# A decoder trunk on one core: S5 tables in other PSUM banks, six norm halves by sums of ones, four smaller moves

## The chip, the cores and the metric

The kernel runs on one core of a Trainium2 chip. The metric is device time in microseconds for one execution. TensorE (PE) has a sequencer and a weight loader of its own (PEld); VectorE (DVE), ScalarE (ACT) and GpSimd (POOL) run beside it, each in its own order, and SyncE (SP) starts most transfers.

## The reference, cut to what matters

Two layers over a sequence of 1024 tokens with 1024 channels, all float32. Each layer is a mixer and a cross-attention over 256 memory tokens, with an RMS norm ahead of each and a residual behind it; a last norm ends the trunk.

```python
def rms_norm(x, g):
    xf = x.astype(jnp.float32)
    y = xf * lax.rsqrt(jnp.mean(xf * xf, axis=-1, keepdims=True) + EPS)
    return (y * g.astype(jnp.float32)).astype(x.dtype)
...
def spatial_gating(u, v, ln_g, ln_b, w_s, b_s):
...
    vn = ((vf - mu) * lax.rsqrt(var + EPS) * ln_g.astype(jnp.float32) + ln_b.astype(jnp.float32)).astype(v.dtype)
```

The first layer's mixer runs dilated attention (16 heads, three patterns) and trailing pools, gates both, and projects 2048 channels back to 1024. The second layer's mixer runs a spatial gating unit (C) and an S5 state-space layer with a GLU (D), gates both, and projects 1536 channels back.

## The kernel before

Everything is held transposed: channels on the 128 partitions, tokens along the free dimension, in two halves of 512 tokens (h is 0 or 1). A float32 product is made of three matmuls on split operands: ACT rounds the operand to its high part (`hilo`, `split`), DVE subtracts to get the low part, and PE adds high x high, high x low and low x high (`mm3`, L206 to L208). So each weight tile `wst` that SP loads becomes `wh` by ACT and `wl` by DVE, and each activation tile becomes a pair.

The stages follow one another on PE: the fold of the memory tokens into the cross-attention weights and the load of x (0 to 200 us); AB, the projections and the attention of the first layer with the pools at its end (200 to 929); its output projection `out_proj` (929 to 1110); cross-attention 0 (to 1290); CD (to 1724); its output projection (to 1860); cross-attention 1 and the last norm (to 2057). While AB runs, a side generator, `s5_prep`, makes the tables of S5 for four groups d: POOL builds a factor W in some 11 us of tensor operations, PE transposes it in two halves (L1154), ACT copies each half out of PSUM to `s5wz` (L1155), PE multiplies it with 16 columns (L1160), DVE masks that to `ktr` (L1165), POOL's queue stores both. The recorded order of each engine is fixed when the kernel is built, and an engine waits for semaphores in that order.

PSUM has four tags with two banks each: `mm`, `s`, `o`, `t`. The tag `mm` holds projections; in AB, `s` holds scores (L536), `t` the transposes of the probabilities (L567, L570), `o` the attention's values (L593, L605). A bank comes free when the engine that reads it is done.

The norm of the next stage is collected while a stage ends. POOL adds squares into `acc` (`norm_sq`). `later` then queues two steps that `flush` runs between projections: `norm_cols` sums over the channels with four matmuls of one column each (L297, a float32 matmul, recorded twice) and gets the factors with ten operations of four columns on DVE (L300 to L306). For CD the factor is wanted along the free dimension too, so `norm_rep` makes four diagonal blocks on DVE (L313), spreads them with a float32 matmul of 512 columns (L314) and copies them to `R` by ACT (L317). In CD, `xd` (L1314) multiplies each projection by `R`.

In `out_proj`, `g_load` (L746) fetches the gated mixer output that was stored to DRAM, and `hilo` splits it to `gr`. In `cd_main` eight tiles `vh` are normalised (L1359) ahead of the gates `ug` (L1367). At the end `norm_rep` gets the factors of the last 256 tokens and `finish` (L285) applies them.

Of the kernel before, what the change touches and what calls it, by code (L numbers as in the profile page):

```python
# [16 lines left out]
EPS = 1e-6  # L17
# [81 lines left out]
class Prog:  # L99
# [164 lines left out]
    def later(s, st, h):  # L264

        s.todo.append(lambda: None)

        def end():
            if st["g"] in (G_X0, G_X1):
                s.norm_cols(st, s.Rt[:, 4 * h:4 * h + 4], 4)  # L270
            else:
                s.norm_rep(st, s.Rt[:, 4 * h:4 * h + 4], s.R[h])
        s.todo.append(end)
# [15 lines left out]
    def norm_cols(s, st, out, n):  # L289
# [10 lines left out]
        V.tensor_scalar(v, p[:, :n], 1.0 / 1024, EPS, op0=ALU.mult, op1=ALU.add)  # L300

        V.tensor_scalar(y.bitcast(mybir.dt.int32), v.bitcast(mybir.dt.int32), -0.5, 1597463007.0, op0=ALU.mult, op1=ALU.add)
        for i in range(3):
            V.tensor_tensor(q, y, y, op=ALU.mult)
            V.scalar_tensor_tensor(q, v, -0.5, q, op0=ALU.mult, op1=ALU.mult)
            V.scalar_tensor_tensor(out if i == 2 else y, q, 1.5, y, op0=ALU.add, op1=ALU.mult)  # L306

    def norm_rep(s, st, Rt, R, n=4):

        s.norm_cols(st, Rt, n)  # L310
        p, d = s.ps("t"), s.u("diag")
        for j in range(n):
            s.nc.vector.tensor_scalar(d[:, 128 * j:128 * j + 128], s.ident, Rt[:, j:j + 1], None, op0=ALU.mult)  # L313
        s.nc.tensor.matmul(p[:, :128 * n], lhsT=s.onef, rhs=d[:, :128 * n], start=True, stop=True)  # L314
        if R is None:
            return p[:, :128 * n]
        s.nc.scalar.activation(R, p[:, :128 * n], AF.Copy)  # L317
# [110 lines left out]
    def load_x(s):  # L428

        s.xg = {}  # L430
        for h in range(2):
# [6 lines left out]
            s.norm_rep(st, s.Rt[:, 4 * h:4 * h + 4], s.R[h])  # L438
# [3 lines left out]
    def proj(s, key, h, held):  # L442
# [6 lines left out]
        if h == 1:  # L449
            s.free(key)  # L450
            del held[key]
            s.flush()
# [224 lines left out]
    def ab_main(s):  # L677
# [15 lines left out]
    def ab_pool(s, gi):  # L693
# [36 lines left out]
        H, L = s.get(key)  # L730
        for d2 in range(2):
# [18 lines left out]

    def out_proj(s, name, KT, gain, get_x, tag):

        s.gr = {}
        todo = [(k, h) for h in range(2) for k in range(KT)]
# [41 lines left out]
    def cross(s, l, gain, tag, save=True):  # L796
# [60 lines left out]
        for si, (h, c0, w) in enumerate(segs):  # L857
            st = {"g": gain}
            fin = {}
            for ct in range(8):  # L860
# [35 lines left out]
                else:  # L896
                    s.norm_sq(st, ct, x, w, last=(ct == 7))
                    nc.scalar.activation(x, x, AF.Copy, scale=s.gains[:, 8 * gain + ct:8 * gain + ct + 1])
                yield 1
# [16 lines left out]
    def s5_prep(s):  # L916
# [224 lines left out]
        zero = s.keep("zero", 128)  # L1141
        V.memset(zero, 0.0)
        for d in range(4):
# [7 lines left out]
            for j in range(2):  # L1151
                p = s.ps("t")
# [5 lines left out]
            p = s.ps("s")  # L1158
# [10 lines left out]
            nc.gpsimd.dma_start(s.s5k[d][128:], zero)  # L1169
# [135 lines left out]
    def cd_main(s):  # L1305
# [52 lines left out]
        for tt in range(8):  # L1358
            V.tensor_scalar(vh[tt], vh[tt], mv[:, 2 * tt:2 * tt + 1], rs[:, tt:tt + 1], op0=ALU.subtract, op1=ALU.mult)  # L1359
        wt, bias = s.sgu  # L1360
        for ct in range(8):
            uu, gg = {}, {}
            for j, dst in ((ct, uu), (8 + ct, gg)):
                for h in range(2):
# [197 lines left out]
```

## Time and profile before

| | |
|---|---|
| three runs | 2055.49, 2062.45, 2062.06 us (median 2062.06) |
| profiled execution | 2059.17 us |
| its span | 2057.4 us, mean granted PE clock 0.997 |
| busy PE, DVE, ACT, POOL | 2020.7, 1102.9, 800.2, 539.9 us |
| PE idle in the span | 36.7 us |

The profiled execution lies between the runs, and 1.8 us of it lie outside the span. Every difference is worked out within the span. PE's busy time counts the pipelined length of each matmul, so back-to-back matmuls of 512 columns start 0.23 us apart though each is shown as 0.39 us.

### The profile page before, as it was taken

How to read it: one execution, taken by the hardware profiler on the slowest of the kernel's cores; microseconds unless marked ns; L12 is line 12 of the kernel's file. 1: busy time of each engine (PE TensorE's matmuls, PEld its weight loads, DVE VectorE, ACT ScalarE, POOL GpSimd, SP SyncE). 2: the span in 40 equal slices, each digit the busy share in tenths (PEclk: the TensorE clock that was granted, in tenths of full speed). 3: DMA queues.
4: the chain of work that ended last, by engine and by line, in shares of the span. 5: the costliest groups of instructions: out<-in, count | busy, mean ns of one | idle time of the engine just before them, and what ended most of it. 6: DMA issues, size and time to landing. Idle time of an engine off the chain costs nothing.

```text
span 2057.4 us, 31828 instructions
## 1 busy us (share of the span) xinstructions
PE 2020.7 (98%) x12350; PEld 1680.1 (82%) x12350; DVE 1102.9 (54%) x1987; ACT 800.2 (39%) x1618; POOL 539.9 (26%) x802
## 2 busy tenths in 40 slices
PE   8999999999999999999999999999999999999998
PEld 7999877777777777888888888888888887888887
DVE  6665055655566675555544555444654334555544
ACT  7666134455344453114433444122221122434453
POOL 5332007922334274221111013221221101210013
PEclk9999999999999999999999999999999999999999
DMA  8889202213122122136533145523321226541142
GB/s 297 300 276 321 93 22 75 73 52 113 54 74 89 59 77 98 70 115 237 186 133 130 42 159 179 164 82 98 121 90 67 80 84 197 197 154 62 67 159 83
DMA packets 129159, 258.68 MB, mean 126 GB/s; under 512 B 12784, under 2 KB 58992, under 8 KB 129008
## 3 DMA queue, kind: packets, MB, share of 16 engines
q1 hardware_dynamic: 86608, 189.52, 27.4%
q0 software_dynamic: 13440, 43.53, 5.7%
q10 hardware_dynamic: 28960, 23.60, 3.6%
q8 instruction: 97, 1.59, 0.3%
q14 instruction: 54, 0.44, 0.1%
HBM read 193.16 MB, written 63.44 MB: 125 GB/s over the span
## 4 chain that ended last, share of the span: by engine, by line
PE 86%; DVE 5%; ACT 2%; issue 1%; DMA 1%; POOL 1%; DVEq 0%; ACTq 0%; POOLq 0%
PE ps_mm L206 13%; PE ps_mm L207 13%; PE ps_mm L208 13%; PE ps_s L207 4%; PE ps_s L208 4%; PE ps_s L206 4%; PE ps_o L208 3%; PE ps_o L207 3%; PE ps_o L206 3%; PE ps_s L536 2%; PE ps_mm L1340 1%; PE ps_mm L1338 1%; PE ps_mm L1339 1%; PE ps_o L593 1%; PE ps_mm L472 1%
## 5 line engine op out<-in xcount | busy, mean ns | idle before, releaser
L181 DVE TENSOR_TENSOR wl<-wst,wh 128x1024 fp32r<-128x1024 f32 (+1 forms) x263 | 346.2, 1330 | 101.9 <-ACT wh L180 97.6
L206 PE MATMUL ps_mm<-xg,wh 128*128 128x512 f32 x928 | 369.9, 399 | 1.3 <-DVE ug L1367 1.0
L207 PE MATMUL ps_mm<-xg,wh 128*128 128x512 f32 x928 | 362.7, 391 | 0.0
L208 PE MATMUL ps_mm<-xg,wl 128*128 128x512 f32 x928 | 362.1, 390 | 0.0
L180 ACT ACTIVATE wh<-wst 128x1024 fp32r<-128x1024 f32 (+1 forms) x263 | 262.6, 1017 | 105.0 <-PE ps_mm L207 84.7
L206 PEld LDWEIGHTS ps_mm<-xg,wh 128*128 128x128 f32 x928 | 174.4, 188 | 47.8 <-issue 10.3
L208 PEld LDWEIGHTS ps_mm<-xg,wl 128*128 128x128 f32 x928 | 174.3, 188 | 36.9
L207 PEld LDWEIGHTS ps_mm<-xg,wh 128*128 128x128 f32 x928 | 174.7, 188 | 33.8 <-issue 0.2
L243 POOL TENSOR_TENSOR acc<-acc,sq 128x512 f32<-128x512 f32 (+1 forms) x81 | 102.3, 1263 | 214.9 <-ACT sq L239 207.8
L226 ACT ACTIVATE xg<-x,gains 128x512 fp32r<-128x512 f32 x64 | 46.2, 722 | 243.5 <-DVE x L782 186.5
L548 ACT ACTIVATE P<-P,mx 128x192 f32<-128x192 f32 (+7 forms) x128 | 66.1, 517 | 155.2 <-DVE mx L547 154.7
L580 ACT ACTIVATE PTr<-ps_t 128x128 f32<-128x128 f32 (+2 forms) x192 | 40.6, 268 | 120.3 <-DVE PT L576 117.9
L543 DVE TENSOR_TENSOR P<-ps_s,cst 128x320 f32<-128x320 f32 (+7 forms) x128 | 65.5, 549 | 21.2 <-PE ps_s L536 9.7
L227 DVE SCALAR_TENSOR_TENSOR xg<-x,gains,xg 128x512 fp32r<-128x512 f32 x64 | 51.7, 807 | 42.9 <-ACT xg L226 42.9
L1367 DVE TENSOR_TENSOR ug<-ps_mm,R 128x512 f32<-128x512 f32 x32 | 22.1, 689 | 90.4 <-PE ps_mm L208 90.3
L576 DVE TENSOR_TENSOR PT<-ps_t,cst 128x256 f32<-128x256 f32 (+1 forms) x128 | 46.4, 400 | 44.4 <-PE ps_t L570 38.6
L207 PE MATMUL ps_s<-gr,wh 128*128 128x512 f32 x168 | 65.6, 390 | 2.1 <-DVE gr L214 2.1
L206 PE MATMUL ps_s<-gr,wh 128*128 128x512 f32 x168 | 65.5, 390 | 1.2 <-ACT gr L213 1.2
L208 PE MATMUL ps_s<-gr,wl 128*128 128x512 f32 x168 | 65.4, 389 | 0.0
L550 ACT ACTIVATE P<-P,den 128x192 f32<-128x192 f32 (+7 forms) x128 | 61.4, 511 | 6.2 <-DVE den L549 6.0
L239 ACT ACTIVATE sq<-x 128x512 f32<-128x512 f32 (+1 forms) x77 | 44.8, 582 | 42.6 <-DVE x L890 37.9
L536 PE MATMUL ps_s<-kk,q 64*32 64x256 f32 (+7 forms) x2048 | 58.4, 332 | 0.9 <-DVE ktr L1165 0.9
(424 smaller groups left out, 4841.8 us busy)
## 6 DMA issues: line engine op xcount, KB each, us to landing
wst<-w_ab SPq DMA_DIRECT2D x40, 512.0 KB, 3.6
wst<-w_out_ab SPq DMA_DIRECT2D x32, 512.0 KB, 4.2
wst<-vsc SPq DMA_DIRECT2D x32, 512.0 KB, 4.4
wst<-w_kv SPq DMA_DIRECT2D x31, 512.0 KB, 7.0
wst<-w_cd SPq DMA_DIRECT2D x24, 512.0 KB, 3.3
wst<-w_out_cd SPq DMA_DIRECT2D x32, 384.0 KB, 3.4
wst<-w_q SPq DMA_DIRECT2D x16, 512.0 KB, 8.4
msc<-mo ACTq DMA_DIRECT2D x32, 256.0 KB, 6.4
```

The lines of the kernel that those rows point to most:

```text
L180: s.last_hi = s.nc.scalar.activation(H[:, :w], t[:, :w], AF.Copy)
L181: s.nc.vector.tensor_tensor(L[:, :w], t[:, :w], H[:, :w], op=ALU.subtract)
L206: s.nc.tensor.matmul(ps, lhsT=lh, rhs=rh, start=(i == 0), stop=False)
L207: s.nc.tensor.matmul(ps, lhsT=lh, rhs=rl, start=False, stop=False)
L208: s.nc.tensor.matmul(ps, lhsT=ll, rhs=rh, start=False, stop=(i == n - 1))
L227: nc.vector.scalar_tensor_tensor(L, x, g, H, op0=ALU.mult, op1=ALU.subtract)
L243: nc.gpsimd.tensor_tensor(st["acc"][:, :n], st["acc"][:, :n], q[:, :n], op=ALU.add)
L536: i = nc.tensor.matmul(p[e][32 * r:32 * r + 32, c], lhsT=q[rows[e], 128 * b + 32 * r:128 * b + 32 * r + 32], rhs=x, start=True, stop=True)
L543: nc.vector.tensor_tensor(t[:, :n], p[e][:, :n], s.cst[:, m0:m0 + n], op=ALU.add)
L548: j = nc.scalar.activation(t[:, :m], t[:, :m], AF.Exp, bias=mx, accum_out=den)
L550: k = nc.scalar.activation(t[:, :m], t[:, :m], AF.Copy, scale=den)
L576: nc.vector.tensor_tensor(PT[b // 2, e][:, c0 + 128 * j0:c0 + 256].rearrange("p (j i) -> p j i", i=128), src, s.cst[:, C_NM + 128 * j0:C_N ...
```

## The change

Six edits stand together.

- S5's transposes and its product of 16 columns go to the tag `o`, where the attention's values are, instead of `t` and `s`. The zero half of each stored table comes from the free columns of `ktr`; four stores of zeros at the start are gone.
- Six norm halves (cross 0, CD and cross 1, h 0 and 1) are summed by `norm_sum`: `acc` is split to high and low, two matmuls of 512 columns with a matrix of ones leave the sum on all partitions, and DVE takes the root there (`rsqrt`, ten operations of 512 columns for CD). The four-column factors come from the diagonal of that sum.
- `g_ahead` loads and splits three `gr` before the last pool and before the last GLU tile; AB's first value projections may use the banks of `mm`, `s` and `o`.
- Four of the eight `vh` are normalised ahead of the gates, the others two at a time between the first gates. In CD a `flush` comes ahead of each `xd`.
- The four loads of the memory tokens are started by ACT instead of SP.
- The last factors use ACT's Sqrt, DVE's reciprocal and one Newton step; a Sqrt of one column (`root`) stands two tiles ahead of them.

```diff
     def later(s, st, h):
-        s.todo.append(lambda: None)
-
-        def end():
-            if st["g"] in (G_X0, G_X1):
-                s.norm_cols(st, s.Rt[:, 4 * h:4 * h + 4], 4)
-            else:
-                s.norm_rep(st, s.Rt[:, 4 * h:4 * h + 4], s.R[h])
-        s.todo.append(end)
+        if not (st["g"] == G_CD and h):
+            s.todo.append(lambda: None)
+        s.todo.append(lambda: s.norm_sum_pe(st))
+        s.todo.append(lambda: s.norm_sum_end(st, s.Rt[:, 4 * h:4 * h + 4], None if st["g"] in (G_X0, G_X1) else s.R[h]))
...
+    def rsqrt(s, v, q, y, out, steps=3):
+        V = s.nc.vector
+        if steps == 3:
+            V.tensor_scalar(y.bitcast(mybir.dt.int32), v.bitcast(mybir.dt.int32), -0.5, 1597463007.0, op0=ALU.mult, op1=ALU.add)
+        for i in range(steps):
+            V.tensor_tensor(q, y, y, op=ALU.mult)
+            V.scalar_tensor_tensor(q, v, -0.5, q, op0=ALU.mult, op1=ALU.mult)
+            V.scalar_tensor_tensor(out if i == steps - 1 else y, q, 1.5, y, op0=ALU.add, op1=ALU.mult)
...
+    def norm_sum_pe(s, st):
+        nc = s.nc
+        p = s.ps("t")
+        h, l = s.u("acch", F32R), s.u("accl", F32R)
+        s.hilo(h, l, st["acc"])
+        nc.tensor.matmul(p, lhsT=s.ones, rhs=h, start=True, stop=False)
+        nc.tensor.matmul(p, lhsT=s.ones, rhs=l, start=False, stop=True)
+        st["sum"] = p
+
+    def norm_sum_end(s, st, Rt, R):
+        nc = s.nc
+        V = nc.vector
+        p = st["sum"]
+        v, q = s.u("nv"), s.u("nt")
+        V.tensor_scalar(v, p, 1.0 / 1024, EPS, op0=ALU.mult, op1=ALU.add)
+        if R is not None:
+            s.rsqrt(v, q, R, R)
+        eye = bass.AP(tensor=s.ident.tensor, offset=s.ident.offset, ap=[s.ident.ap[0], [0, 4], [1, 128]])
+        V.tensor_tensor(q.rearrange("p (j i) -> p j i", j=4), v.rearrange("p (j i) -> p j i", j=4), eye, op=ALU.mult)
+        c = s.col("rc", 16)
+        V.tensor_reduce(c[:, 0:4], q.rearrange("p (j i) -> p j i", j=4), axis=AX.X, op=ALU.add)
+        s.rsqrt(c[:, 0:4], c[:, 4:8], c[:, 8:12], Rt)
...
+        if out is None:
+            nc.scalar.activation(y, v, AF.Sqrt)
+            V.reciprocal(y, y)
+            s.rsqrt(v, q, y, y2, 1)
...
-            nc.sync.dma_start(s.memx[j // 2][:, c], s.a["memT"][:, 512 * j:512 * j + 512])
+            nc.scalar.dma_start(s.memx[j // 2][:, c], s.a["memT"][:, 512 * j:512 * j + 512])
...
+                s.mtags = ("mm",) if pr else ("mm", "s", "o")
                 yield from s.ab_v(pr // 4)
+                s.mtags = ("mm",)
...
+    def g_ahead(s):
+        s.gr = {}
+        for k in range(3):
+            s.g_load(k, 0)
...
-                p = s.ps("t")
+                p = s.ps("o")
                 for g in range(4):
                     nc.tensor.transpose(p[:, 128 * g:128 * g + 128], W[:, 512 * j + 128 * g:512 * j + 128 * g + 128], s.ident)
                 nc.scalar.activation(wz[:, 512 * j:512 * j + 512], p, AF.Copy)
                 yield 1
             nc.gpsimd.dma_start(tab[0], wz)
-            p = s.ps("s")
+            p = s.ps("o")
...
-            nc.gpsimd.dma_start(s.s5k[d][128:], zero)
+            V.memset(ktr[:, 128:256], 0.0)
+            nc.gpsimd.dma_start(s.s5k[d][128:], ktr[:, 128:256])
...
+                    with s.tc.issue_after(s.anchor.ins):
+                        while left and len(left) > 4 - 2 * (2 * (dst is gg) + h):
+                            t8 = left.pop(0)
+                            V.tensor_scalar(vh[t8], vh[t8], mv[:, 2 * t8:2 * t8 + 1], rs[:, t8:t8 + 1], op0=ALU.subtract, op1=ALU.mult)
```

Three places of the built order show what moves. The first is PE in AB, where the first half of table 0 is transposed (L1154 before, L1193 after) and a block's probabilities follow (L567 and L570 before, L597 and L600 after); the twelve matmuls of a projection between them are left out. Before:

```order
L1154 MATMUL ps_t_5695<-cst_84,s5W_5513 128x128 [waits Activation_49,Pool_49]
L1154 MATMUL ps_t_5695<-cst_84,s5W_5513 128x128 x3
...
L567 MATMUL ps_t_5705<-cst_84,P_5548 128x128 [waits Activation_49]
L570 MATMUL ps_t_5705<-cst_84,P_5548 128x128 x2
L567 MATMUL ps_t_5713<-cst_84,P_5557 128x128 [waits Activation_49]
```

After, at the same place:

```order
L1193 MATMUL ps_o_5693<-cst_84,s5W_5511 128x128 [waits Pool_49]
L1193 MATMUL ps_o_5693<-cst_84,s5W_5511 128x128 x3
...
L597 MATMUL ps_t_5703<-cst_84,P_5546 128x128 [waits Activation_49]
L600 MATMUL ps_t_5703<-cst_84,P_5546 128x128 x2
L597 MATMUL ps_t_5711<-cst_84,P_5555 128x128 [waits Activation_49]
```

The transposes keep their place but have left the bank that the probabilities need: before, the last row waits for ACT's copy of the table half (`s5wz`), after it for ACT's copy of older probabilities (`PTr`), and the table no longer waits for ACT.

The second place is DVE at the start of CD, second half of the tokens. R_80 is the factor of the first 512 tokens, R_81 that of the second; each `xd` frees the bank of one projection. Before:

```order
L1314 TENSOR_TENSOR xd<-ps_mm,R_80 128x8x64 [waits PE_49]
L181 TENSOR_TENSOR wl<-wst,wh 128x1024 [waits DMAHW6_49,Activation_49]
L300 TENSOR_SCALAR rc<-ps_t 128x4 [waits PE_49]
...
L313 TENSOR_SCALAR diag<-cst,Rt 128x128 [waits DMASW3_49,DVE_49]
L313 TENSOR_SCALAR diag<-cst,Rt 128x128 x3
L1314 TENSOR_TENSOR xd<-ps_mm,R_80 128x8x64 [waits PE_49]
L1314 TENSOR_TENSOR xd<-ps_mm,R_81 128x8x64 [waits Activation_49]
```

After:

```order
L1355 TENSOR_TENSOR xd<-ps_mm,R_80 128x8x64 [waits PE_49]
L181 TENSOR_TENSOR wl<-wst,wh 128x1024 [waits DMAHW6_49,Activation_49]
L315 TENSOR_SCALAR nv<-ps_t 128x512 [waits DMASW1_49,PE_49]
L289 TENSOR_SCALAR R_81<-nv 128x512 [waits DVE_49]
L291 TENSOR_TENSOR nt<-R_81 128x512 [waits DMASW4_49,DVE_49]
...
L292 SCALAR_TENSOR_TENSOR nt<-nv,nt 128x512 [waits DVE_49]
L1355 TENSOR_TENSOR xd<-ps_mm,R_80 128x8x64 [waits PE_49]
L293 SCALAR_TENSOR_TENSOR R_81<-nt,R_81 128x512 [waits DVE_49]
L319 TENSOR_TENSOR nt<-nv,cst 128x512 [waits DVE_49]
L1355 TENSOR_TENSOR xd<-ps_mm,R_81 128x8x64
```

Ten operations of 512 columns (`nv`, the first guess, and eight of the nine steps) now stand ahead of the second `xd` with R_80, where ten of four columns and four of 128 stood.

The third place is ACT at the end of the GLU, where `sg` is the GLU's sigmoid and `gr` the high part of the mixer output. Before:

```order
L1414 ACTIVATE sg<-ps_s 128x512 [waits DMASW2_49,PE_49]
L1414 ACTIVATE sg<-ps_s 128x512 [waits DVE_49,PE_49]
L213 ACTIVATE gr<-gst 128x512 [waits DMAHW4_49]
L213 ACTIVATE gr<-gst 128x512 [waits DMAHW5_49]
L213 ACTIVATE gr<-gst 128x512 [waits DMAHW6_49]
```

After:

```order
L1460 ACTIVATE sg<-ps_s 128x512 [waits PE_49,Pool_49]
L213 ACTIVATE gr<-gst 128x512 [waits DMAHW3_49,DVE_49]
L213 ACTIVATE gr<-gst 128x512 [waits DMAHW4_49,DVE_49]
L213 ACTIVATE gr<-gst 128x512 [waits DMAHW5_49,DVE_49]
L1460 ACTIVATE sg<-ps_s 128x512 [waits DVE_49,PE_49]
L1460 ACTIVATE sg<-ps_s 128x512 [waits DMASW3_49,DVE_49,PE_49]
```

Three `gr` have moved ahead of the last two sigmoids.

## Rows read from the trace of the kernel before

**Rows 1.** The page, busy time: engine, us (share of span), instructions.

```profile
PE 2020.7 (98%) x12350; PEld 1680.1 (82%) x12350; DVE 1102.9 (54%) x1987; ACT 800.2 (39%) x1618; POOL 539.9 (26%) x802
```

**Rows 2.** PE's waits: what waited for whom: us in total, times, longest.

```profile
PE ps_t L567 <- ACT s5wz L1155: 5.1, 2, 3.5
...
PE ps_s L206 <- ACT mg L226: 2.1, 1, 2.1
...
PE ps_s L536 <- DVE ktr L1165: 0.9, 1, 0.9
```

**Rows 3.** Timeline of ACT, first 13 us: start, us, operation [idle before, releaser].

```profile
9.08 0.63 ACT L171 ACTIVATE wh<-wst 128x512 fp32r<-128x512 f32 x1 [2.40 <-DMA wst<-w_kv]
...
10.22 0.89 ACT L226 ACTIVATE mg<-mem,gains 128x256 fp32r<-128x256 f32 x2
```

**Rows 4.** Timeline of SP, first 13 us.

```profile
2.68 0.43 SPq L158 DMA_DIRECT2D wst<-w_kv  x1
```

**Rows 5.** Windows in AB: PE, PEld, DVE, ACT, POOL busy (instructions), PE clock, DMA, GB/s.

```profile
490.60:494.00 3.40, 1.39 (x35) 0.80 (x35) 1.72 (x3) 3.33 (x9) 0.00 (x0) 1.00 0.00 1
494.04:497.45 3.41, 3.41 (x36) 2.89 (x28) 1.81 (x4) 0.47 (x3) 0.00 (x0) 0.50 0.37 116
...
695.43:698.84 3.41, 3.41 (x34) 2.11 (x35) 1.60 (x3) 0.00 (x0) 3.18 (x4) 0.50 0.08 24
```

**Rows 6.** Timeline of PE in AB: twelve matmuls in two blocks, and table 1.

```profile
494.06 1.97 PE L593 MATMUL ps_o<-PT,V 128*64 128x128 f32 x12
...
542.47 1.09 PE L593 MATMUL ps_o<-PT,V 128*64 128x128 f32 x12
...
563.28 0.63 PE L1154 MATMUL ps_t<-cst,s5W 128*128 128x128 f32 x4 [2.39 <-ACT PTr L580]
```

**Rows 7.** Timeline of POOL at table 1, where factor W is finished.

```profile
558.59 3.24 POOL L938 TENSOR_TENSOR s5W<-s5W,s5w 128x1024 f32<-128x1024 f32 x1
```

**Rows 8.** Timeline of PE at the norm of CD, first half.

```profile
1255.54 0.95 PE L297 MATMUL ps_t<-onef,acc 128*128 128x1 f32 x8
1256.35 0.48 PE L206 MATMUL ps_s<-pt,wh 128*128 128x512 f32 x1
...
1264.39 1.02 PE L314 MATMUL ps_t<-diag,onef 128*128 128x512 f32 x2
1264.84 0.80 PE L208 MATMUL ps_o<-pt,wl 128*128 128x512 f32 x1
```

**Rows 9.** Timeline of PE at the start of CD.

```profile
1307.24 1.02 PE L314 MATMUL ps_t<-diag,onef 128*128 128x512 f32 x2
1308.56 0.50 PE L206 MATMUL ps_mm<-xg,wh 128*128 128x512 f32 x1 [0.30 <-DVE xd L1314]
```

**Rows 10.** Timeline of DVE at the start of CD.

```profile
1307.44 1.07 DVE L1314 TENSOR_TENSOR xd<-ps_mm,R 128x512 f32<-128x512 f32 x1 [2.52 <-PE ps_mm L208]
```

**Rows 11.** Groups of DVE's operations by form: times, busy us, mean ns, idle before.

```profile
L257 DVE TENSOR_SCALAR nv<-ps_t 128x512 f32<-128x512 f32 x1 | 0.7, 692 | 0.3 <-PE ps_t L254 0.3
```

**Rows 12.** Timeline of PE: both output projections begin, first gates of CD, the end.

```profile
930.94 0.50 PE L207 MATMUL ps_s<-gr,wh 128*128 128x512 f32 x1 [0.99 <-DVE gr L214]
...
1456.87 0.50 PE L206 MATMUL ps_mm<-xg,wh 128*128 128x512 f32 x1 [1.04 <-DVE ug L1367]
...
1725.98 0.50 PE L206 MATMUL ps_s<-gr,wh 128*128 128x512 f32 x1 [1.20 <-ACT gr L213]
...
1728.04 0.50 PE L207 MATMUL ps_s<-gr,wh 128*128 128x512 f32 x1 [1.08 <-DVE gr L214]
...
2050.19 0.93 PE L314 MATMUL ps_t<-diag,onef 128*128 128x256 f32 x2 [2.73 <-DVE diag L313]
```

**Rows 13.** Timeline of DVE at the first gates of CD.

```profile
1449.21 5.87 DVE L1359 TENSOR_SCALAR vh<-vh,stats 128x1024 f32<-128x1024 f32 x8
```

**Rows 14.** Timeline of DVE at the end.

```profile
2047.49 0.16 DVE L300 TENSOR_SCALAR rc<-ps_t 128x2 f32<-128x2 f32 x1 [1.37 <-PE ps_t L297]
...
2049.45 0.16 DVE L306 SCALAR_TENSOR_TENSOR rl<-rc 128x2 f32<-128x2 f32 x1
```

More of the change, by code (lines that the diff above doesn't have):

```diff
@@ L287, in finish, with norm_sum, norm_cols @@
                                                      x[:, :2 * w].rearrange("p (c n) -> p c n", c=2))
-    def norm_cols(s, st, out, n):
+    def rsqrt(s, v, q, y, out, steps=3):
[6 more added lines that the diff above has]
+            V.scalar_tensor_tensor(out if i == steps - 1 else y, q, 1.5, y, op0=ALU.add, op1=ALU.mult)
+    def norm_sum(s, st, Rt, R=None):
+        s.norm_sum_pe(st)
+        s.norm_sum_end(st, Rt, R)
+    def norm_sum_pe(s, st):
[19 more added lines that the diff above has]
+        s.rsqrt(c[:, 0:4], c[:, 4:8], c[:, 8:12], Rt)
+    def norm_cols(s, st, n, out=None):
         nc = s.nc
@@ L300, in norm_cols @@
         V.tensor_scalar(v, p[:, :n], 1.0 / 1024, EPS, op0=ALU.mult, op1=ALU.add)
[L302 to L310, printed above, removed]
+        y2 = y if out is None else out
+        if out is None:
+            nc.scalar.activation(y, v, AF.Sqrt)
+            V.reciprocal(y, y)
+            s.rsqrt(v, q, y, y2, 1)
+        else:
+            s.rsqrt(v, q, y, y2)
         p, d = s.ps("t"), s.u("diag")
         for j in range(n):
[L313 to L317, printed above, removed]
+            V.tensor_scalar(d[:, 128 * j:128 * j + 128], s.ident, y2[:, j:j + 1], None, op0=ALU.mult)
+        nc.tensor.matmul(p[:, :128 * n], lhsT=s.onef, rhs=d[:, :128 * n], start=True, stop=True)
+        return p[:, :128 * n]
     def constants(s):
@@ L437, in load_x @@
                 yield 1
-            s.norm_rep(st, s.Rt[:, 4 * h:4 * h + 4], s.R[h])
+            s.nc.scalar.activation(s.R[h], s.norm_cols(st, 4, s.Rt[:, 4 * h:4 * h + 4]), AF.Copy)
             yield 1
@@ L451, in proj @@
             del held[key]
-            s.flush()
         s.last = p
@@ L730, in ab_pool @@
         H, L = s.get(key)
+        if gi == 3:
+            s.g_ahead()
         for d2 in range(2):
@@ L749, in g_load @@
         s.gr[k, h] = (t[:, :512], t[:, 512:])
+    def g_ahead(s):
+        s.gr = {}
+        for k in range(3):
+            s.g_load(k, 0)
     def out_proj(s, name, KT, gain, get_x, tag):
-        s.gr = {}
-        todo = [(k, h) for h in range(2) for k in range(KT)]
+        todo = [(k, h) for h in range(2) for k in range(KT) if (k, h) not in s.gr]
         per = KT // 2
@@ L898, in cross @@
                     nc.scalar.activation(x, x, AF.Copy, scale=s.gains[:, 8 * gain + ct:8 * gain + ct + 1])
+                    if si == 2 and ct == 6:
+                        nc.scalar.activation(s.col("root"), st["acc"][:, :1], AF.Sqrt)
                 yield 1
@@ L908, in cross @@
             s.flush()
-            R = s.norm_rep(st, s.col("rl", 16)[:, :2], None, 2)
+            R = s.norm_cols(st, 2)
             for ct in (0, 2, 4, 6):
@@ L1139, in outer @@
             return o
-        zero = s.keep("zero", 128)
-        V.memset(zero, 0.0)
         for d in range(4):
@@ L1313, in cd_main @@
                 yield from s.proj(("cd", 16 + d), h, held)
+                s.flush(1)
                 s.anchor = V.tensor_tensor(x.rearrange("p (j c) -> p j c", j=8)[:, :, 64 * h:64 * h + 64],
@@ L1357, in cd_main @@
         V.scalar_tensor_tensor(rs, q, 1.5, rs, op0=ALU.add, op1=ALU.mult)
-        for tt in range(8):
-            V.tensor_scalar(vh[tt], vh[tt], mv[:, 2 * tt:2 * tt + 1], rs[:, tt:tt + 1], op0=ALU.subtract, op1=ALU.mult)
+        left = list(range(8))
         wt, bias = s.sgu
@@ L1405, in cd_main @@
             H, L = s.get(key)
+            if ot == 3:
+                s.g_ahead()
             gt = s.b("Gd")
```

## The prediction

> **What bounds the kernel now.** I read the busy shares first. PE is busy 98% of the span and no other engine more than 54% [rows 1], so the kernel is a chain of matmuls and the time changes only by what PE is spared: a wait, a matmul, or a stretch at half clock. The 36.7 us that PE idles are the whole pool of waits. The list of PE's waits names them: 5.1 us for ACT's copies of S5's tables, 2.1 for the memory tokens at the start, 0.9 for `ktr` [rows 2]. The timelines give the others: 2.4 at table 1 [rows 6], 1.0, 1.2 and 1.1 where the output projections begin, 1.0 at the first gates, 2.7 at the end [rows 12]. Then the clock: the windows show two stretches of 3.41 us in AB at 0.50, that is 1.2 GHz, while the stretch ahead of the first is at 1.00 with PE busy in only 1.39 of 3.40 us and ACT in 3.33 [rows 5]. Some of that pool can't be reached: PE can't start before its first weights, and the stores behind the last matmul stay.
>
> **The start.** ACT waits 2.40 us for the second half of the first weight tile, rounds it, and only at 10.22 rounds the memory tokens that PE's second group wants [rows 3]. SP had issued that half at 2.68 behind two loads of memory tokens, at 0.43 us an issue [rows 4]; after the change it comes two issues, 0.9 us, earlier. Four stores of zeros go from POOL's queue. Against that ACT now does four issues ahead of its own work, and three squares ahead of the next tokens (0.4 us each by their kind). Above: 0.9 by the issues and the whole 2.1 that PE waited, 3.0. Below: nothing, if the transfers are what is scarce. I take 1.5, between them. The Trainium skill (page "DMA: Bandwidth & Descriptors", section "Issuing engines are not separate DMA queues") says that transfers from different engines share the same 16 DMA engines and interleave, and that a second issuing engine saves only issue time. By that rule the sum would be 0.6 us smaller, for it leaves the 0.9 of issue. The trace can't show it, since before the change SP alone loads tokens and weights.
>
> **S5's tables.** The first order excerpt shows the cause of the 5.1 us: the transposed half lies in a bank of `ps_t`, the probabilities' transposes behind it need that bank, and ACT's copy that frees it stands in ACT's queue behind other work, which is busy without a break meanwhile [rows 5]. In a bank of `ps_o` the copy may be late without PE noticing, as long as the next user of that bank is further away; in the new order 48 or more PE instructions stand between the first half of table 0 and the next. So 5.1 goes, and likewise 0.9 for `ktr`, which held a bank of scores. At table 1, PE waited until 563.28 [rows 6] while W was ready at 561.83 (558.59 + 3.24) [rows 7]. W remains to be waited for, so of 2.4 us at most 1.4 go; the transposes now stand three matmuls (0.7 us) earlier and wait for W there, which leaves 0.7. Sum 6.7. Below: 2, if PE meets the next late copy soon after; above: 7.4. POOL's extra work, a memset and a store for each table, lies after `ktr` where POOL idles.
>
> **The half clock.** Twelve matmuls take 1.97 us in the first slow stretch and 1.09 elsewhere [rows 6]; so 3.41 us there hold 1.9 us of work at full clock, and each stretch costs 1.5. The first follows 3.5 idle us that go, so I count it whole. The second follows only 0.9 of idle and a group of 16-column matmuls that stays; I count half. Sum 2.25; bounds 0 and 3.0.
>
> **Norms.** The group of column sums holds PE from 1255.54 to 1256.35 and the next matmul is shown 0.09 longer than the usual 0.39 [rows 8]: 0.90. Two matmuls of 512 columns at 0.23 cost 0.45. Each of the six halves so saves 0.45, 2.7 together. The spreading matmul of CD's first half holds PE from 1264.39 to 1264.84 and makes the next one 0.41 longer [rows 8]: 0.86 more. In the second half it hides in a wait: PE goes from 1307.24 to 1308.56 [rows 9] because the bank comes free only when `xd` is done, 1307.44 + 1.07 [rows 10]. That wait stays, so nothing is saved there. Sum 3.6.
>
> What this adds is DVE time, and it is paid only if an `xd` comes late (second excerpt). Counting back from 1307.24 at 0.23 for 24 matmuls and 0.9 for the column sums, the projection ahead ended at 1300.9. In the new order the sum's second matmul stands 8 matmuls ahead of that end, so `nv` starts near 1299.9, on this trace's clock with the two new matmuls in. Ten operations at 0.69 [rows 11] end at 1306.8; the `xd` behind them can't start before its projection, near 1307.0. It fits with 0.2 us to spare. Were each operation 0.1 slower it would cost 0.8, and the next `xd` with R_81, some 3.5 us behind, still has a projection of 5.4 us as cover. I take 0; bounds: a gain of 0 here and a loss of 1.5.
>
> **Seams.** The first `gr` waits 0.99 at the one projection, 1.20 and 1.08 at the other [rows 12], since ACT's roundings stood behind the last sigmoid, which waits for PE (third excerpt). Three ready pairs cover 18 to 27 matmuls, 4 to 6 us, and a pair costs ACT and DVE about 0.6 to 0.7 each. Sum 3.3; below 2.2, if the early loads hold up the last sigmoids for 1.1. The value projections in three tags cure nothing: PE has no wait there. **The gates:** DVE is at `vh` for 5.87 us [rows 13] while a bank waits; half of it ahead saves 2.9, more than the 1.04 that PE waited [rows 12]. Sum 1.0. **Restarts:** after each of seven such waits the first matmul is shown as 0.50 instead of 0.39 [rows 12], 0.7 together.
>
> **The end.** Ten operations stand from 2047.69 to 2049.65, 0.2 apart [rows 14]. Now there are a hop to ACT and back, a reciprocal and three more. Four at 0.2 leave 1.1 for the hop; I give it 0.4 to 0.8, as this trace has no Sqrt of two columns on the path, and save 0.5 (bounds 0 and 0.8). The extra Sqrt two tiles ahead lets the table load fall before the last sums; no other load stands behind it.
>
> **Sum.** 1.5 + 6.7 + 2.25 + 3.6 + 3.3 + 1.0 + 0.7 + 0.5 = 19.6 us. The profiled execution of 2059.17 becomes 2039.6. The median of the runs is 2.9 higher and the lowest run 3.7 lower; the four executions have a mean of 2059.8, and I name 2040. By the lower bounds (0, 2, 0, 2.1, 2.2, 0.5, 0.3, 0) the gain is 7, by the upper (3.0, 7.4, 3.0, 3.6, 3.3, 1.0, 0.7, 0.8) 23.
>
> **Rivals.** 0.5% is 10.3 us, about what a measurement of this kernel can tell from no change.
>
> *The waits come back.* ACT works without a break just where PE waited [rows 5], and DVE and ACT must still handle each block of probabilities. If PE, freed from the table's bank, meets the block's own copies, two thirds of S5's 6.7 return (4.5), and with the idle the slow clock (2.25): 2040 + 6.8 = 2047. For it: ACT's 3.33 of 3.40 us. Against: after table 0 PE runs without a wait of a microsecond until table 1.
>
> *The sums' operands come late.* The split of `acc` needs POOL, then ACT, then DVE, whose queues hold weights; the new matmuls stand inside a projection and stop it. At 0.7 us for each of six halves, the length of one DVE operation, 4 us are lost: 2044.
>
> *The shared transfers.* By rows 3 the second weight half decides ACT's order; if it lands no earlier, as when eight transfers share the bandwidth, the start gives nothing: 2041.5. This is the mechanism behind the rule cited above.
>
> *The moves don't do what they say.* The slow stretches stay, the seams wait for the loads instead, the start gives nothing and half of S5's waits return: 20 - 2.25 - 3.3 - 1.5 - 3.4 = 9.6 of gain, 2050 or more, within 0.5%.
>
> *Slower.* The tables now sit in the banks of the attention's values. There are twelve groups (three for each of four tables); if each holds up the values by one late ACT copy, as the longest of before (3.5 us, rows 2), PE loses 12 x 3.5 = 42 and the time is 2082. It decides above 20/12 = 1.7 us a group for no gain, and 2.5 for slower by 10.3. Against it stands the distance to the next user in the order.
>
> **How the numbers follow.** Forecast 0.55, waits back 0.17, late operands 0.08, shared transfers 0.10, moves without effect 0.06, slower 0.04. The forecast's own range is 2036 to 2045, from the runs' spread of 3.5 us either way. The whole range goes from 2034 (upper bounds, less the spread) to 2053 (waits back with the same spread, and a part of the case within 0.5%). Faster by over 0.5% means under 2051.8: the forecast, late operands, shared transfers and half of waits back with what lies clearly under, 0.82; the same 0.14; slower 0.04.
>
> **What would show it.** PE's list of waits without `s5wz`, `ktr` and, at the two seams, `gr`; about 1 us for W at table 1; the clock row at 1.00 through AB; column sums left only in the prologue and at the end; PE's wait ahead of the second projection of CD's d = 1 still near 1.3 us. It would be wrong if other names take their place in that list, above all values behind `s5wz`, or matmuls of ones behind `accl`, or if PE's first groups start as late as before.

## The result, and the profile after

The changed kernel takes 2036.29 us (median of 4 runs, 2035.2 to 2037.6) and the kernel before, beside it, 2061.56 (4 runs, 2055.49 to 2062.45). The ratio is 0.9884, 95% interval 0.9864 to 0.9904: faster by 25.3 us by the medians. The profiled execution took 2035.66 with a span of 2034.0, 23.4 less than before.

The page of the changed kernel, first busy times (to be read against [rows 1]), then the granted clock in 40 slices, in tenths:

```profile
PE 2009.1 (99%) x12310; PEld 1674.5 (82%) x12310; DVE 1125.8 (55%) x2011; ACT 803.2 (39%) x1625; POOL 538.4 (26%) x805
...
PEclk9999999999999999999999999999999999999999
```

PE is busy 11.6 us less and idles 24.9 us instead of 36.7, so half of the gain is idle time and half is work that became shorter: fewer matmuls for the norms, and no matmuls at half clock. DVE is busy 23 us longer, with the wide norms. The one place where PE could have paid for that is CD's first `xd`; the hole in PE's work there is 1.3 us long before and after. PE's list of waits answers to [rows 2]:

```profile
PE ps_s L206 <- ACT wh L171: 6.3, 1, 6.3
PE ps_s L206 <- ACT mg L226: 2.3, 1, 2.3
PE ps_t L347 <- DVE diag L346: 1.8, 1, 1.8
PE ps_o L1193 <- POOL s5W L979: 1.8, 1, 1.8
...
PE ps_mm L206 <- DVE xd L1355: 1.2, 1, 1.2
...
PE ps_o L1193 <- ACT s5wz L1194: 0.7, 1, 0.7
```

The 5.1 us for ACT's table copies (`s5wz`) are down to 0.7, and `ktr`, `gr` and `ug` are gone. The memory tokens (`mg`), W at table 1 and CD's `xd` still stand. The windows of AB (first stretch where table 0 is transposed, then AB as a whole; columns as in [rows 5]) have no stretch at half clock:

```profile
490.08:493.48 3.40, 2.66 (x19) 2.08 (x16) 1.14 (x3) 2.36 (x7) 0.00 (x0) 1.00 0.21 77
...
199.84:915.84 716.00, 710.25 (x5601) 566.53 (x5600) 406.13 (x871) 281.17 (x713) 279.22 (x529) 1.00 0.25 81
```

The timeline of PE: table 0, table 1, the first output projection, a norm of CD, the start of CD, the second output projection, the end.

```profile
491.09 0.66 PE L1193 MATMUL ps_o<-cst,s5W 128*128 128x128 f32 x4 [0.74 <-ACT s5wz L1194]
...
555.16 0.66 PE L1193 MATMUL ps_o<-cst,s5W 128*128 128x128 f32 x4 [1.76 <-POOL s5W L979]
...
915.62 0.39 PE L208 MATMUL ps_mm<-plr,wl 128*128 128x512 f32 x1
915.84 0.39 PE L206 MATMUL ps_s<-gr,wh 128*128 128x512 f32 x1
916.07 0.39 PE L207 MATMUL ps_s<-gr,wh 128*128 128x512 f32 x1
...
1244.21 0.39 PE L305 MATMUL ps_t<-accl,ones 128*128 128x512 f32 x1
1244.45 0.39 PE L208 MATMUL ps_s<-pt,wl 128*128 128x512 f32 x1
...
1291.40 0.50 PE L206 MATMUL ps_mm<-xg,wh 128*128 128x512 f32 x1 [1.16 <-DVE xd L1355]
...
1705.59 0.39 PE L206 MATMUL ps_s<-gr,wh 128*128 128x512 f32 x1
1705.81 0.39 PE L207 MATMUL ps_s<-gr,wh 128*128 128x512 f32 x1
...
2027.01 0.70 PE L347 MATMUL ps_t<-diag,onef 128*128 128x256 f32 x2 [1.79 <-DVE diag L346]
```

The `gr` matmuls follow each other at 0.23 where [rows 12] had 0.99, 1.20 and 1.08 of waiting. Each of the two matmuls of ones for a norm half is one more matmul of 0.24, in the middle of a projection (`accl` at 1244.21, the next at 1244.45), where the column sums took 0.81 [rows 8]. The last matmuls wait 1.79 instead of 2.73.

To see where the 23.4 us came from, the span is divided at the starts of four matmuls that every kernel here has in PE's timeline: the first of AB's projections, the first `gr` matmul of each output projection, and the last matmul. The rows below the changed kernel are the experiments; their times beside the kernel before follow with each.

| kernel | span | start | AB | first to second `gr` | to the last matmul |
|---|---|---|---|---|---|
| before | 2057.4 | 201.39 | 727.95 | 796.64 | 324.53 |
| changed | 2034.0 | 199.84 | 716.00 | 789.75 | 321.74 |
| s5_back | 2048.5 | 201.19 | 729.21 | 789.73 | 321.74 |
| s5_only | 2045.9 | 200.26 | 717.47 | 796.43 | 324.79 |
| ktr_s | 2038.6 | 201.16 | 718.22 | 790.31 | 322.02 |
| mg_first | 2037.5 | 200.99 | 717.84 | 789.76 | 322.02 |
| start_back | 2037.6 | 202.49 | 716.49 | 789.70 | 322.04 |
| norms_back | 2038.7 | 201.09 | 716.40 | 791.93 | 322.69 |
| seams_back | 2037.2 | 199.12 | 716.26 | 792.44 | 322.69 |
| best | 2036.8 | 200.54 | 719.63 | 788.15 | 321.78 |
| cd_tags | 2033.5 | 199.80 | 717.11 | 788.19 | 321.77 |

So the gain is 1.55 at the start, 11.95 in AB, 6.89 and 2.79 in the two stages behind it, and 0.3 from the start of the last matmul on. The stages behind AB repeat within 0.6 us wherever an edit doesn't touch them; the start varies by 2 us between executions of the same code.

AB can be divided further, for the matmuls of its projections stand in the same order in both kernels. Taking the start of one such matmul behind each table, counted from the beginning of AB in its own kernel, gives what was gained up to there; the last column sorts the prediction's terms for S5's tables and for the half clock by the table at which they fall.

| behind | before | changed | gained up to here | gained at this table | forecast |
|---|---|---|---|---|---|
| table 0 | 530.07 | 523.49 | 5.03 | 5.03 | 3.5 + 1.5 = 5.0 |
| table 1 | 590.00 | 582.12 | 6.33 | 1.30 | 0.7 |
| table 2 | 659.97 | 649.51 | 8.91 | 2.58 | 1.6 |
| table 3 | 711.98 | 698.52 | 11.91 | 3.00 | 0.9 + 0.75 = 1.65 |

In all the rest of AB the two kernels differ by 0.04 us.

### The profile page after: what moved, and what is told of

Same layout as the page of the kernel before. It is cut to its first block, busy times and chain, and to the rows that moved or that the text cites. A ratio compares the mean times of both kernels' runs of the same rounds, so it can differ in the third digit from the quotient of the medians.

```text
span 2034.0 us, 31775 instructions
## 1 busy us (share of the span) xinstructions
PE 2009.1 (99%) x12310; PEld 1674.5 (82%) x12310; DVE 1125.8 (55%) x2011; ACT 803.2 (39%) x1625; POOL 538.4 (26%) x805
## 4 chain that ended last, share of the span: by engine, by line
PE 93%; DVE 3%; DMA 1%; ACT 1%; issue 1%; POOL 1%; ACTq 0%; SPq 0%; DVEq 0%; POOLq 0%
PE ps_mm L206 14%; PE ps_mm L208 14%; PE ps_mm L207 14%; PE ps_s L207 5%; PE ps_s L208 5%; PE ps_s L206 5%; PE ps_o L207 4%; PE ps_o L206 4%; PE ps_o L208 4%; PE ps_s L566 2%; PE ps_mm L1379 1%; PE ps_mm L1381 1%; PE ps_mm L1380 1%; PE ps_o L623 1%; PE ps_o L882 1%; PE ps_o L880 1%
## 5 line engine op out<-in xcount | busy, mean ns | idle before, releaser
L213 ACT ACTIVATE pt<-ps_t 128x128 fp32r<-128x128 f32 x128 | 34.7, 276 | 66.4 <-DVE pt L214 45.4
```

## The experiments

The first theory is the prediction's own: PE loses what it waits for, and banks held by ACT's late copies, with the slow clock behind them, are the largest part. Each experiment undoes or repeats one part.

**s5_back: the tables return to `t` and `s`.**

```diff
-                p = s.ps("o")
+                p = s.ps("t")
...
-            p = s.ps("o")
+            p = s.ps("s")
```

> The changed kernel with S5's transposes back in the tag t and its 16-column product back in s; everything else stays. First theory (the table banks alone make what AB gained, about 12 us of the 23): PE's waits for ACT's table copies come back with some 5 us, at least one stretch of AB is at half clock again, and the span is 2044 to 2047. Rival (the other edits shifted the phase of AB, so that the waits would be gone in the old banks as well): under 2 us for the copies, no half clock, span under 2038.

It took 2050.03 us (2049.78 to 2050.33), ratio 0.9943 (0.9928 to 0.9958); its span of 2048.5 is a little over the expected. PE's waits:

```profile
PE ps_t L597 <- ACT s5wz L1194: 5.2, 2, 3.5
PE ps_t L1193 <- ACT PTr L610: 2.7, 2, 2.5
...
PE ps_s L566 <- DVE ktr L1204: 0.9, 1, 0.9
```

and three windows at half clock, one more than before the change:

```profile
492.55:495.96 3.41, 3.41 (x43) 1.77 (x45) 0.85 (x2) 1.64 (x6) 0.00 (x0) 0.50 0.20 77
564.23:567.64 3.41, 3.41 (x11) 2.52 (x9) 0.49 (x3) 3.40 (x9) 0.00 (x0) 0.50 0.01 5
697.35:700.76 3.41, 3.41 (x18) 2.56 (x9) 3.13 (x3) 0.00 (x0) 3.41 (x4) 0.50 0.08 24
```

AB is 13.2 us longer; behind it nothing moves, and the start stays within its spread. The new stretch stands behind the 2.5 us wait at table 1; the same wait of 2.39 in the kernel before [rows 6] had none behind it.

**s5_only: the same two lines alone, in the kernel before.**

```diff
-                p = s.ps("t")
+                p = s.ps("o")
...
-            p = s.ps("s")
+            p = s.ps("o")
```

> The kernel before with nothing changed but the tags of S5's transposes and product. First theory (the parts add up): AB is 11 to 12 us shorter, no half clock in it, span 2045 to 2047, and the waits at the seams, the norms and the gates are as before. Rival (the gain needs the other edits too): span above 2050.

It took 2049.77 us (2047.6 to 2050.25), ratio 0.9942 (0.9926 to 0.9959). AB falls by 10.5 us, of which no other edit has a share, with the clock at 1.00 throughout. Behind table 3 it is 11.4 us ahead of the kernel before, where the changed kernel is 11.9; another 0.9 is lost between 760 and 800 us, where no edit stands and where `cd_tags` below loses the same 0.9 against the changed kernel. Its list of waits has two sorts side by side, those of the seams and gates that these lines don't touch, and the table's, which they do:

```profile
PE ps_s L207 <- DVE gr L214: 2.1, 2, 1.1
...
PE ps_mm L206 <- DVE ug L1367: 1.0, 1, 1.0
PE ps_o L1154 <- ACT s5wz L1155: 0.8, 1, 0.8
```

Two words in the code are thus worth about half of the change. They act in two ways that these runs don't part: the tag decides which bank is held, and the built order changes with it. The product of 16 columns, for one, stands ahead of a projection under `o` (498.85 at table 0 in the changed kernel) and in the middle of one under `s` (510.47 before).

**ktr_s: only the product of 16 columns returns to `s`.**

```diff
-            p = s.ps("o")
+            p = s.ps("s")
```

> The changed kernel with only the 16-column product back in a bank of scores. First theory (the second slow stretch of before hangs on the wait for that bank): PE waits 0.9 us for ktr at table 3, the clock falls to 0.5 for 3.41 us behind it, span 2036.5 to 2037.5. Rival (that stretch came from where the group happened to stand): at most the wait comes back, no half clock, span 2034 to 2035.5.

One run: 2040.29, span 2038.6. The wait is back (PE's timeline), the slow stretch is not (the window that ends where the wait ends, and one that reaches 2.4 us beyond it):

```profile
686.96 0.98 PE L566 MATMUL ps_s<-kk,q 64*32 64x256 f32 x30 [0.77 <-DVE ktr L1204]
```

```profile
683.56:686.96 3.40, 2.63 (x22) 2.12 (x20) 2.57 (x11) 0.74 (x3) 0.00 (x0) 1.00 0.00 0
...
686.00:689.40 3.40, 2.63 (x38) 1.75 (x38) 2.28 (x10) 0.00 (x0) 2.20 (x4) 1.00 0.08 24
```

Here the theory fell: the slow stretch that it expected didn't come. The second slow stretch of before doesn't follow from that wait alone. The rival has the clock right, but the span lies above both expectations: AB is 2.2 us longer and begins 1.3 later, the latter within the spread of the start. Matmul by matmul, AB's 2.2 are 1.3 at table 3, where the wait is, and 0.15, 0.3 and 0.4 at tables 0, 1 and 2, where the product has gone back into the middle of a projection; 0.2 of table 1's share is a longer wait for W. So the product's tag is worth about 1.9 us without any slow stretch, not the 0.9 of its wait.

**mg_first: the memory tokens that PE's second group wants are rounded ahead of the second weight half.**

```diff
-        nc.scalar.activation(H, x, AF.Copy, scale=g)
+        s.hi_ins = nc.scalar.activation(H, x, AF.Copy, scale=g)
...
-                s.split(0, k // 2 - 1)
+                if k == 4:
+                    with s.tc.issue_after(s.hi_ins.ins):
+                        s.split(0, 1)
+                else:
+                    s.split(0, 0)
```

> The changed kernel with ACT's order at the start altered: the tokens for PE's second group are rounded ahead of the second half of the first weight tile. First theory (the first 140 us are set by the stream of weights, so what PE gains ahead of it is given back): PE's second group starts near 8.5 us instead of 10.57, the first projection of AB still at 199.6 to 200.0, span 2033.5 to 2034.5. Rival (PE's start counts): the first projection of AB near 198, span 2032.

One run: 2039.2, span 2037.5. PE's second group now starts at 8.14 us instead of 10.57, but AB begins at 200.99, not earlier than elsewhere: what PE gains at 8 us it waits for again behind it (0.48 and 0.50 us for later tokens, 0.75 for a weight at 29.8). AB is 1.84 longer, for the wait at table 1 had a slow stretch behind it this time (PE's timeline, then the window):

```profile
556.45 0.66 PE L1197 MATMUL ps_o<-cst,s5W 128*128 128x128 f32 x4 [1.93 <-POOL s5W L983]
...
562.73 0.66 PE L1197 MATMUL ps_o<-cst,s5W 128*128 128x128 f32 x4
```

```profile
557.87:561.28 3.41, 3.41 (x10) 2.53 (x9) 0.54 (x3) 3.38 (x8) 0.00 (x0) 0.50 0.33 132
```

This prices a slow stretch directly. Between the two rows stand the same matmuls as between these two of the changed kernel:

```profile
555.16 0.66 PE L1193 MATMUL ps_o<-cst,s5W 128*128 128x128 f32 x4 [1.76 <-POOL s5W L979]
...
559.87 0.66 PE L1193 MATMUL ps_o<-cst,s5W 128*128 128x128 f32 x4
```

They take 6.28 us here and 4.71 there, so the stretch costs 1.57 us, close to the prediction's 1.5. The wait itself is 0.17 longer than the changed kernel's, and the last 0.1 of the 1.84 stands elsewhere in AB.

**start_back: memory tokens on SP's queue and the stores of zeros at the start, as before.**

```diff
-            nc.scalar.dma_start(s.memx[j // 2][:, c], s.a["memT"][:, 512 * j:512 * j + 512])
+            nc.sync.dma_start(s.memx[j // 2][:, c], s.a["memT"][:, 512 * j:512 * j + 512])
...
+        zero = s.keep("zero", 128)
+        V.memset(zero, 0.0)
...
-            V.memset(ktr[:, 128:256], 0.0)
-            nc.gpsimd.dma_start(s.s5k[d][128:], ktr[:, 128:256])
+            nc.gpsimd.dma_start(s.s5k[d][128:], zero)
```

> The changed kernel with its start undone: SP starts the memory tokens' loads again and POOL stores the four zero blocks. First theory (the start gives nothing; the first projection of AB came between 199.8 and 201.4 us whichever start a kernel had): it comes between 199.5 and 201.5 here, span 2033 to 2036. Rival (the start is worth the 1.5 us that were forecast): 201.4 or later, and later than every kernel with the new start.

One run: 2039.3, span 2037.6. AB begins at 202.49, the latest of all, as the rival said. What makes it late stands in PE's timeline 110 us behind the edit:

```profile
118.47 0.39 PE L206 MATMUL ps_o<-mg,wh 128*128 128x256 f32 x1 [0.83 <-ACT wh L180]
120.03 0.39 PE L208 MATMUL ps_o<-mg,wl 128*128 128x256 f32 x1 [1.06 <-DVE wl L181]
```

with a window at 0.50 from 120.46 to 123.87. The kernel before waits at the same place, 0.69 us for `wl` at 119.47; the changed kernel doesn't. But neither goes with the start alone: `s5_only` has the old start and no wait there, `s5_back` has the new one and waits 0.40 at 119.72. Over the profiled executions, seven with the new start (without `mg_first`) have AB begin at 199.12 to 201.19 (mean 200.39), three with the old one at 200.26 to 202.49 (mean 201.38). The means differ by 1 us. At the price of 1.57 found in `mg_first`, the slow stretch in one of the three executions alone makes about half of that. That the new start gains anything is not shown.

**norms_back: the six halves are summed by columns again** (the old functions in place of `norm_sum_pe` and `norm_sum_end`).

```diff
-        if not (st["g"] == G_CD and h):
-            s.todo.append(lambda: None)
-        s.todo.append(lambda: s.norm_sum_pe(st))
-        s.todo.append(lambda: s.norm_sum_end(st, s.Rt[:, 4 * h:4 * h + 4], None if st["g"] in (G_X0, G_X1) else s.R[h]))
+        s.todo.append(lambda: None)
+
+        def end():
+            if st["g"] in (G_X0, G_X1):
+                s.cols_old(st, s.Rt[:, 4 * h:4 * h + 4], 4)
+            else:
+                s.rep_old(st, s.Rt[:, 4 * h:4 * h + 4], s.R[h])
+        s.todo.append(end)
```

> The changed kernel with the six norm halves summed and spread as before; all else stays. First theory (each half costs PE 0.45 more, and CD's first half 0.86 for its spreading matmul): PE loses 3.0 to 3.6 us between the first output projection and the end, span 2037 to 2038.5, time 2039 to 2040. Rival (the split sums stop PE inside projections and give part of it back, or the wide chain on DVE does): under 1.5 us of difference.

It took 2040.4 us (2040.33 to 2040.83), ratio 0.99 (0.9883 to 0.9916). The two stages behind AB are 2.18 and 0.95 longer, 3.1 together: the theory holds.

**seams_back: the three `gr` of each seam are again loaded behind the last gate.**

```diff
-            s.g_ahead()
...
-        todo = [(k, h) for h in range(2) for k in range(KT) if (k, h) not in s.gr]
+        s.gr = {}
+        todo = [(k, h) for h in range(2) for k in range(KT)]
```

> The changed kernel without the product that is put ahead at the two seams (the first gate's half product of the out projection stands behind its whole eviction again); all else as in the changed kernel. First theory (each seam was a wait of 1.0 to 1.2 us, and the work that fills it was there anyway): the waits of 1.15, 1.36 and 1.24 us stand again at the seams, from table 1's first out projection on both seams together cost 3.3 to 3.8 us, span 2037.5 to 2040.5 less what the start and AB vary by, about 1 us either way. Rival (the filled seams only moved the wait to the next bank): the stages lose under 1.5 us in all, and span 2034 to 2036.

It took 2041.36 us (2038.95 to 2044.49), ratio 0.9906 (0.9882 to 0.9929). PE's timeline has the three waits of [rows 12] again, to the hundredth for two of them (the 1.15, 1.36 and 1.24 of the expectation count the same waits from 0.23 behind the start of the matmul ahead, not from its shown end at 0.39):

```profile
916.99 0.50 PE L207 MATMUL ps_s<-gr,wh 128*128 128x512 f32 x1 [0.99 <-DVE gr L214]
...
1707.82 0.50 PE L206 MATMUL ps_s<-gr,wh 128*128 128x512 f32 x1 [1.21 <-ACT gr L213]
...
1709.88 0.50 PE L207 MATMUL ps_s<-gr,wh 128*128 128x512 f32 x1 [1.08 <-DVE gr L214]
```

The stages behind AB are 2.69 and 0.95 longer, 3.6 together: the theory holds, and the work that fills the seams costs nothing in AB (716.26 here, 716.00 with it).

Together `norms_back` and `seams_back` account for 2.18 + 2.69 of the 6.89 us that the stage between the two output projections gained. The 2.02 that are left belong to the edits of CD, the `vh` and the gates, for which no run was made; in the two timelines they stand between 1440 and 1510 us on the clock of the kernel before.

**best: table 1's transposes one step later, and CD's first x projections in the banks of `mm` and `o` in turn,** to remove the two waits that are left.

```diff
+            if d == 1:
+                yield 1
...
+            s.mtags = ("mm", "o") if d < 2 else ("mm",)
```

> The changed kernel with two more moves: table 1's transposes one step of the side generator later, and CD's first two projection pairs in the banks of mm and o instead of mm alone. First theory (these are the two longest waits left in the middle): the 1.8 us for W at table 1 and the 1.2 us for xd go, no half clock in AB, span 2030 to 2031.5, time near 2033. Rival (the waits only move to the next user of a bank or to the next table): span 2033.5 or more.

It took 2038.45 us (2036.58 to 2038.88), ratio 0.9888 (0.9873 to 0.9903): no better than the changed kernel, and its span of 2036.8 is the rival's: the waits moved. CD gained 1.6 us and the wait for W fell to 0.7, but AB became 3.6 longer. PE's timeline and DVE's show the new wait:

```profile
744.76 0.50 PE L206 MATMUL ps_mm<-xg,wh 128*128 128x512 f32 x1 [3.05 <-DVE gb L758]
```

```profile
735.10 1.01 DVE L573 TENSOR_TENSOR P<-ps_s,cst 128x384 f32<-128x384 f32 x2
736.03 6.92 DVE L576 TENSOR_TENSOR P<-P 128x128 f32<-128x128 f32 x2
742.88 0.73 DVE L577 TENSOR_REDUCE mx<-P 128x1 f32<-128x256 f32 x2
```

Two small DVE operations, usually 0.48 us a pair, take 6.92. POOL's own timeline, of which the first two rows and the last of its chain of products stand here, has work from 735.70 to 742.80 without a break, the issue of one store among the products:

```profile
735.70 1.04 POOL L979 TENSOR_TENSOR s5w<-Er,trig 128x512 f32<-128x512 f32 x1
736.68 0.60 POOL L651 DMA_DIRECT2D gab<-G  x1
...
741.55 1.25 POOL L979 TENSOR_TENSOR Ei<-s5w,s5w 128x512 f32<-128x512 f32 x1
```

DVE's pair ends 0.15 us behind POOL's last product. The Trainium skill (page "SBUF — State Buffer", section "Who interferes with whom") says that VectorE and GpSimd share one pair of ports, that a VectorE instruction with two SBUF inputs contends there with a GpSimd instruction that reads SBUF, and that the lock on the pair is exclusive, the one that issues first blocking the other. This trace agrees, as far as an end 0.15 us behind POOL's last product shows it, with DVE's pair standing over several of POOL's instructions in a row. Shorter cases stand in the other traces: in the kernel before such a pair takes 3.21 us from 698.31 while POOL works until 701.17, in the changed kernel 2.05 from 685.68 while it works until 687.38, and both end 0.35 us behind POOL. The step that moved the transposes moved POOL's and DVE's work against each other, and `gb`, behind the blocked pair, held PE's bank. That POOL's work is the cause was read from the traces and not tried by itself.

**cd_tags: the second line of `best` alone.**

```diff
+            s.mtags = ("mm", "o") if d < 2 else ("mm",)
```

> The changed kernel with one line more: the first two pairs of CD's x projections of both directions take their groups from the PSUM tags mm and o in turn instead of mm alone. Theory (the 1.3 us that PE waits at CD's start stands because the first xd evictions hold mm's two banks; AB's longer time in the kernel that combined this with moved transposes came from the transposes): the wait at CD's start goes, from the first out projection of table 1 to that of table 2 takes 788.0 to 788.6 us instead of 789.75, AB stays at 716 to 718.5, span 2032 to 2035. Rival (the banks of o are then missing elsewhere, the wait moves on as it did in AB): CD takes 789.5 us or more, with a wait of 0.8 us or more on a bank of o, span 2034.5 to 2038.

It took 2035.74 us (2034.92 to 2036.23), ratio 0.9873 (0.9854 to 0.9892), span 2033.5. The wait at CD's start is gone (PE's timeline: two projections follow each other at 0.22):

```profile
1290.88 0.39 PE L208 MATMUL ps_o<-xg,wl 128*128 128x512 f32 x1
1291.10 0.39 PE L206 MATMUL ps_mm<-xg,wh 128*128 128x512 f32 x1
```

CD's stage takes 788.19 instead of 789.75, 1.56 less, as the theory had it, and again as in `best`. In the total that can't be told from the changed kernel: the two ratios' intervals overlap for the most part. AB took 717.11 here against 716.00 without any edit in it, 0.9 of the 1.1 between 760 and 800 us, so that one profile of AB isn't good to better than 1 us unless the place of the difference is known.

## Why the prediction was right

Forecast were 2040 us and a gain of 19.6 in the profiled execution; measured were 2036.3 and 23.4 (25.3 by the medians). The direction and the places held, and for the tables, the norms and the seams the mechanism was shown by undoing them. Two terms, the tables and the gates, were sized too small; the start's term agrees only by luck.

- **S5's tables and the half clock: 6.7 + 2.25 = 8.95 forecast, 11.95 measured in AB, 10.5 and 13.2 by the two experiments.** The waits went as forecast (5.1 to 0.7, `ktr` gone, W at table 1 still 1.76 where 1.7 was left over; the list of signs had said about 1). The price of a slow stretch was right too, 1.57 us where 1.5 was taken. What was too small shows where AB is divided by S5's tables: table 0 came out as forecast. At table 3 the second stretch went whole where it had been counted half: 0.8 us more. And the product of 16 columns was worth more than its wait of 0.9: `ktr_s` loses about 1.9 by it over the four tables, without a slow stretch: 1.0 more. That is 1.8 of the 3.0 that were missing; the other 1.2 was not separated. `ktr_s` doesn't give the second stretch back with the wait, so why it came is open.
- **Rival "the waits come back":** in a small way only. At table 0 a wait for `s5wz` of 0.74 remains, now in the values' bank. The slower rival wanted 1.7 us a group in twelve groups; there is one of 0.7.
- **Norms: 3.6 forecast, 3.1 measured.** The last stage's two halves gave the 0.9 that was forecast (0.95), the four halves and the spreading matmul of the stage ahead of it gave 2.18 instead of 2.66. The rival "the sums' operands come late" didn't happen: the rows at 1244 show no wait. The wide DVE chain fits with 0.05 us to spare, where 0.2 had been worked out. In DVE's timeline of the changed kernel its tenth operation is followed by `xd` without idle time:

```profile
1289.51 0.69 DVE L292 SCALAR_TENSOR_TENSOR nt<-nv,nt 128x512 f32<-128x512 f32 x1
1290.28 1.07 DVE L1355 TENSOR_TENSOR xd<-ps_mm,R 128x512 f32<-128x512 f32 x1
```

  `xd` starts at 1290.28, and the projection that it reads ends at 1289.86 + 0.39 = 1290.25. PE's hole behind that projection stays at 1.3 us, as forecast; it is shown as a wait of 1.16 now and was one of 0.30 [rows 9], for the spreading matmul that used to fill the rest is gone.
- **Seams and restarts: 3.3 and 0.7 forecast.** The seams measure 3.6 with the restarts that belong to them.
- **The gates: 1.0 forecast, 2.0 by what the experiments leave over.** The wait for `ug` of 1.04 is gone. The step counted this one wait alone; 1.3 us are gained where it stood and 0.7 some 45 us behind it, among matmuls of S5 that no term names. No run undoes this edit by itself.
- **The end: 0.5 forecast, 0.94 measured.** The hop to ACT and back, put at 0.4 to 0.8, takes 0.27 beyond DVE's operations:

```profile
2025.26 0.16 DVE L335 TENSOR_SCALAR rc<-ps_t 128x2 f32<-128x2 f32 x1 [1.37 <-PE ps_t L332]
2025.69 0.17 DVE L340 RECIPROCAL rc<-rc 128x2 f32<-128x2 f32 x1 [0.27 <-ACT rc L339]
```

- **The start: 1.5 forecast, 1.55 in this pair, by luck.** The step said that the second weight half and with it PE's second group come earlier. The half did so in this pair (ACT's timeline, against 9.08 in [rows 3]):

```profile
8.27 0.63 ACT L171 ACTIVATE wh<-wst 128x512 fp32r<-128x512 f32 x1 [1.97 <-DMA wst<-w_kv]
...
10.02 1.69 ACT L226 ACTIVATE mg<-mem,gains 128x256 fp32r<-128x256 f32 x4
```

  but ACT then does its squares and the tokens are rounded only at 10.02 against 10.22; PE's wait for `mg` is 2.27 where it was 2.1, and its second group starts at 10.57 against 10.77, nearly as late as before, which the prediction had named as a sign of being wrong. Nor does the earlier half follow from the edit: `s5_only` and `start_back`, with the old start, round it at 7.97 and 8.19, the eight kernels with the new start at 7.22 to 8.63. `mg_first` takes most of PE's wait away and gains nothing. So the rival "shared transfers" (start worth nothing, 2041.5) isn't excluded; the 1.55 is smaller than the 2 us by which equal starts differ.

## What to carry to other kernels

Where one engine is busy 98% of the time, list its waits, find for each the bank or buffer that is held and by whose late copy, and give the late tile a bank whose next user is far away; here that is two words and half of the gain, two stretches at half clock among it. An edit that shifts side work by a step shifts every engine's work against the others: time it with nothing else in it, as `cd_tags` beside `best` shows. A gain at the very start may be lost again on the way: in `mg_first` PE was 2.4 us ahead at 8 us and not ahead at 200.

## What the runs showed of the hardware that was not expected

- The granted clock doesn't follow the length of a wait alone. It fell to 0.50 behind a wait of 0.88 us for `ktr` before the change (695.43 in [rows 5]) but not behind one of 0.77 in `ktr_s`; behind 1.93 for W at table 1 in `mg_first` but not behind 1.97 to 1.99 there in `norms_back`, `ktr_s` and `start_back`, nor behind 2.39 in the kernel before; and in `best` it stayed at 1.00 behind 3.05 us. The windows of `best`, ahead of that wait's end and behind it:

```profile
741.40:744.80 3.40, 0.35 (x3) 0.04 (x1) 3.06 (x7) 1.48 (x5) 3.40 (x6) 1.00 0.22 81
744.80:748.20 3.40, 2.97 (x12) 2.13 (x12) 2.75 (x8) 3.37 (x5) 1.67 (x7) 1.00 0.61 228
```

  Whether a wait costs a slow stretch, 1.57 us more, can't be told from its length in these traces; what decides it stays open.
- A pair of DVE operations of 0.48 us stood for 6.92 us while POOL worked through a chain of products and one store.
- Executions of the same start differ by 2.1 us in when AB begins, more than the 1.5 that the edit to the start was thought to be worth.
